# A gate chunk's last addition traced two groups behind its product, and transpositions of row sums two groups behind the sums

## The chip, the cores and the metric

The kernel runs on one core of a Trainium2 chip. The metric is the device time of one execution in microseconds: 983.66 us as the median of three executions (983.5 to 984.84).

## The reference, cut to what matters

A two-layer bidirectional encoder over one sequence of 512 tokens with a width of 1024, in fp32. Layer 0 (A here) mixes tokens with dilated sliding-window attention in three dilations and eight heads; layer 1 (B) with grouped-query attention, eight query heads on two key heads, rotary angles over a grid. Both layers attend with four more heads to 256 memory tokens.

```python
h = rmsnorm(x, norm_g[i])
proj = h @ w_in[i]                 # q, k, v heads, memory queries, gate path
o = concat(mixer(q, k, v), memory_attention(qm, mem_h, w_kv[i]))
y = o * silu(gate)
x = x + y @ w_out[i]
```

## The kernel before, in words

**Products.** Each fp32 product is made of three TensorE matmuls of rounded parts (mm3, L162 to L165: high by high, high by low, low by high). Weights come as blocks of 128 x 1024 by DMA (wl) and are split on the chip: ScalarE (ACT) casts the high part wh (L282), VectorE (DVE) subtracts it for the low part wo (L292), four blocks in a ring. Most projections multiply two-by-two blocks with seven products instead of eight, in the function s_chunk. Its products, in order, are 12, 11, S1, S2, S4, S3 and 22; each goes to a PSUM bank, and behind each a copy (keep, L357, on ACT) or an addition (add, L367, on DVE) takes the bank's sum out. One subtraction (L361) stands between: s5 minus s3 is the block 22 of the result, and s5's tile is where it is written; the last addition, of block 21, reads s3 and overwrites it.

**Order.** No scheduler moves anything: each engine runs its instructions in the order in which the program traces them. A Driver object counts groups. A group is twelve matmuls of 128 x 512 or twenty-four of 128 x 256 on one or two weight blocks. Behind a group's matmuls come, in this order, the first steps of the keep and add generators that are due (free), the splits, sums and loads of weights (advance, with its L292 and L282), the release of the group's own bank (with a delay d, counted in groups), and one step of every other running generator (tick). What follows an addition or a subtraction is a generator too, ev: for a gate block the tanh (ACT L722), the product with its argument (DVE L724), the load og of attention outputs from DRAM (L717), the multiplication (L732; for the memory heads' part L735, with a cast L738 and a subtraction L740). A chunk of n=256 (units = 1) has one group per product; there are eleven of them, among them the three gate chunks m, a and b of each layer. A chunk of n=512 has two groups per product.

**Around the change.** At the end of layer A, prep_y forms sums of the gated blocks (ys: L776, L778; yf: L784, L786) and splits them (yS: ACT L759, DVE L760) as right factors of the output projection (out_proj). The last heads' attention outputs are stored to DRAM by put_od (L915) and merged by their weights (L1062 to L1078; ACT's exponential L1067). The output projection's rows go through ev_o: residual and norm (L455), then the first factors of layer B. For its lower half of rows, sum_h (L496) makes the difference xs, and sums_h transposes it on PE (turn4, L461; splits L157 and L160) and makes three more sums (L504 to L506), which rest_h transposes later. The steps of ev_o are EO, in groups. The memory keys of layer B are normed (L519, L524, xn) and transposed (L531, qT) at the same time. In layer B the attention (attn_b: L1304, L1313, L1314, ptb L1323, pbT L1327 and L1332) runs between the groups of the gate chunks; its last outputs are stored to odb and loaded as og.

Of the kernel before, what the change touches and what calls it, by code (L numbers as in the profile page):

```python
# [13 lines left out]
ALU = mybir.AluOpType  # L14
# [12 lines left out]
MEM_STEP = 1, 1  # L27
MEM_D = 4
PD, W_EARLY = (1, 2, 2, 1), True
EO = 1, 2, 1, 1, 1  # L30
YB = {"m": (2, 2), "k": (1, 1, 1), 0: (1, 2, 1), 1: (1, 2, 1)}
Y = [3, 2, 2, 2, 3, 2, 2, 1, 1, 1]

# [91 lines left out]
def trunk_kernel(ctx: ExitStack, tc: tile.TileContext, x, mem, wall, norm_g, mem_norm_g, gcol,  # L125
                 qn_a, kn_a, qn_b, kn_b, ident_d, mask_d, tab_a, tab_b, out):
    nc = tc.nc
    V, A, G, T = nc.vector, nc.scalar, nc.gpsimd, nc.tensor
# [14 lines left out]
    def s2(dt=F32, name="s2"):  # L143
        return pool.tile([128, 512], dt, tag="s2", name=name, bufs=NS2)

    def pj(name="pj"):
        return psum.tile([128, 512], F32, tag="pj", name=name, bufs=4)
# [14 lines left out]
    def mm3(o, lh, ll, rh, rl, start, stop):  # L162
        T.matmul(o, lh, rh, start=start, stop=False, skip_group_check=True)  # L163
        T.matmul(o, lh, rl, start=False, stop=False, skip_group_check=True)  # L164
        T.matmul(o, ll, rh, start=False, stop=stop, skip_group_check=True)  # L165
# [183 lines left out]
    def s_chunk(n, act, ev, tokens=True, pre=None, half=False):  # L349


        units, per = n // 256, 1024 // n
        bank, snap = [None, None], {}

        def keep(name, u, b):
            t = snap[name, u] = s2(name="sn")
            A.copy(t, b)  # L357
            yield 1
            if name == "s3":
                c = snap["s5", u]  # L360
                V.tensor_tensor(c, c, t, ALU.subtract)  # L361
                yield 1
                yield from ev("22", u, c)

        def add(q, name, u, b):
            t = snap[name, u]
            V.tensor_tensor(t, b, t, ALU.subtract if q == "12" else ALU.add)  # L367
            yield 1
            yield from ev(q, u, t)

        after = ((keep, "z"), (add, "11", "z"), (keep, "s5"), (keep, "s2"), (add, "12", "s2"), (keep, "s3"), (add, "21", "s3"))
        for i, (a, s, fresh) in enumerate(PRODUCTS):
            while a not in act:
                drv.tick()
            if fresh:
                bank[s] = [pj() for _ in range(units)]
            for x in range(units):
                wh, wo = [t.rearrange("p (k c) -> p k c", c=n) for t in W.take()]
                ah, al = act[a][:, 0], act[a][:, 1]
                for b in range(2):  # L380
                    if pre and i == x == 0 and b:
                        pre()
                    if half and b:
                        n_half[0] += 1
                        if n_half[0] % half == 0:
                            drv.half()
                    o = bank[s][b] if units == 2 else bank[s][0][:, b * 256:(b + 1) * 256]
                    bs = slice(b * 128, (b + 1) * 128)
                    for k in range(per):
                        kk = x * per + k  # L390
                        st, sp = fresh and kk == 0 and (units == 2 or b == 0), kk == 3
                        if tokens:
                            mm3(o, ah[:, kk, bs], al[:, kk, bs], wh[:, k], wo[:, k], st, sp)
                        else:
                            mm3(o, wh[:, k, bs], wo[:, k, bs], ah[:, kk], al[:, kk], st, sp)
                drv.free()
                W.advance()
                if x == units - 1:
                    f, *arg = after[i]
                    for u in range(units):  # L400
                        d = 2 if f is keep else 2 + u + (units == 1 and i == 6)
                        drv.release(f(*arg, u, bank[s][u]), d)
                drv.tick()

# [35 lines left out]
    def norm_1(xb, both=False):  # L440

        ss = sm(2, "ss")
        for j in range(2):
            jk = s2(name="sq")
            if both and j:
                V.tensor_tensor_reduce(jk, xb[j], xb[j], 1.0 / 1024.0, 0.0, ALU.mult, ALU.add, ss[:, j:j + 1])
            else:
                A.activation(jk, xb[j], AF.Square, scale=1.0 / 32.0, accum_out=ss[:, j:j + 1])
        r, e = sm(1, "rstd"), sm(1, "mse")
        G.tensor_tensor(e, ss[:, 0:1], ss[:, 1:2], ALU.add)  # L450
        return rstd_of(e, 1)

    def norm_2(xb, r, row, js=(0, 1)):
        for j in js:
            V.scalar_tensor_tensor(xb[j], xb[j], r, row[j], ALU.mult, ALU.mult)  # L455
# [38 lines left out]
    def sum_h(low):  # L494
        s1 = s2(name="xs1")
        V.tensor_tensor(s1, low[0], low[1], ALU.subtract)  # L496
        return s1

    def sums_h(H, top, low, c, s1, sums):

        (a11, a12), a21 = top, low[0]
        s2_, s4 = s2(name="xs2"), s2(name="xs4")
        put_h(H, "S1", c, s1)
        V.tensor_tensor(s2_, s1, a11, ALU.subtract)  # L504
        V.tensor_tensor(a21, a11, a21, ALU.subtract)
        V.tensor_tensor(s4, a12, s2_, ALU.add)  # L506
        sums.append((s2_, s4, a21, low[1]))

    def rest_h(H, sums, d=1):
        for i, k in enumerate(("S2", "S4", "S3", "22")):  # L510
            for c in range(2):
                put_h(H, k, c, sums[c][i])
            yield d
# [187 lines left out]
    def gates(od, o_done):  # L701
# [3 lines left out]
        def gate(H, first, g, half=False):  # L705
# [6 lines left out]
            def ev(q, u, t):  # L712
# [29 lines left out]
                if {(2, 0, j), (2, 1, j)} <= y_done:  # L742
                    for k in range(2):
                        ys[2 * j + k] = (yt[j][0][:, k], yt[j][1][:, k])

            s_chunk(256, H, ev, tokens=False, half=half)

        def prep_y():
# [45 lines left out]
    def out_proj(YW, ys, src, evac, tiles, half=False):  # L794

        acc, done = {}, set()

        def load():
            for i in range(2):
                for u, t in enumerate(tiles()):  # L800
                    nc.sync.dma_start(t, src[2 * i + u])
                    acc[2 * i + u] = halves(t)
                yield 2

        def ev(q, u, t):
            b, n = 2 * (int(q[0]) - 1) + u, int(q[1]) - 1
            while b not in acc:
                yield 1
            V.tensor_tensor(acc[b][n], t, acc[b][n], ALU.add)
            done.add((n, b))  # L810

        drv.spawn(load(), ACC_AT)
        s_chunk(512, YW, ev, half=half)
        out_rest(ys, acc, done, evac)
# [89 lines left out]

    drv.spawn(mem_norm(0), MEM_AT)
    s_chunk(512, H, ev_v0, pre=second)
    km, vm = mem_kv(0, Ms[0])

# [256 lines left out]
    def ev_o(n, b, x1):  # L1165
        if n:
            for j in range(2):
                nc.sync.dma_start(x1d[b][:, j * 512:(j + 1) * 512], x1[j])
            r = norm_1(x1)
            yield EO[0]  # L1170
            norm_2(x1, r, rows["x1"])
            x1b[b] = x1
            yield EO[1]
            if b < 2:
                put_h(H2, "12", b, x1[1])
                put_h(H2, "11", b, x1[0])
            else:
                s1 = sum_h(x1)
                yield EO[2]
                sums_h(H2, x1b[b - 2], x1, b - 2, s1, sums_b)  # L1180
            if b == 3:
                yield EO[3]
                yield from rest_h(H2, sums_b, EO[4])

# [306 lines left out]
```

## Time and profile before

| | |
|---|---|
| time, median of three | 983.66 us |
| the profiled execution | 983.88 us |
| its span | 982.1 us |
| PE busy | 951.9 us (97%) |
| DVE busy | 822.1 us (84%) |
| ACT busy | 645.0 us (66%) |
| POOL busy | 333.5 us (34%) |
| DVE, L292, the low parts of weights | 255 x 1233 ns = 312.8 us |
| ACT, L282, the high parts | 255 x 1059 ns = 269.6 us |

Engines in the rows: PE is TensorE, DVE VectorE, ACT ScalarE, POOL GpSimd, SP the engine that issues most DMAs. A row of a timeline has start, duration, engine, line, operation, output and inputs, shapes, and in brackets the idle time before it with what ended it. A duration holds an instruction's whole passage, and the next one on DVE starts some 80 ns before its end. A row of waits has the total, the number and the longest. A row of stretches has the length, then the busy time and number of instructions of PE, PEld, DVE, ACT and POOL, the TensorE clock granted, the DMA share and GB/s.

### The profile page before, as it was taken

What the parts mean: (1) busy time and instruction counts of PE and PEld (TensorE: products, weight loads), DVE (VectorE), ACT (ScalarE), POOL (GpSimd) and SP (SyncE); (2) the same over time, 40 slices, a digit from 0 to 9 for tenths busy, and PEclk for the clock granted to TensorE, in tenths of its full rate; (3) what the DMA queues carried; (4) which work ended last, traced back from release to release, by engine and by line L of the source; (5) the groups of instructions that cost most, each with busy time, mean ns of one, the idle gap of its engine ahead of it and who ended that gap; (6) DMA issues with size and microseconds to landing.
All of it is one profiled execution on the core that took longest, in us unless ns stands there. A gap on an engine that the chain in (4) does not pass through costs nothing.

```text
span 982.1 us, 16662 instructions
## 1 busy us (share of the span) xinstructions
PE 951.9 (97%) x5724; PEld 838.8 (85%) x5724; DVE 822.1 (84%) x1487; ACT 645.0 (66%) x1623; POOL 333.5 (34%) x470
## 2 busy tenths in 40 slices
PE   7999999999999999999999989998999999998998
PEld 4788988888888888888899977886999999996886
DVE  6796788888888888888888998969689998889964
ACT  5555668686767676868676656455677766667650
POOL 1132423556555555554644010123533331011000
PEclk9999999999999999999999999999999999999999
DMA  8989947869686868686949795759695786786332
GB/s 333 309 275 351 239 97 188 290 120 268 154 250 155 250 164 243 158 249 137 271 117 300 228 235 173 258 218 322 181 204 144 196 213 171 227 213 152 129 129 86
DMA packets 86967, 206.13 MB, mean 210 GB/s; under 512 B 25058, under 2 KB 35810, under 8 KB 86883
## 3 DMA queue, kind: packets, MB, share of 16 engines
q1 hardware_dynamic: 70034, 146.28, 43.0%
q0 software_dynamic: 15552, 56.63, 30.5%
q10 hardware_dynamic: 1296, 2.16, 0.6%
q8 instruction: 45, 0.74, 0.3%
q14 instruction: 40, 0.32, 0.1%
HBM read 157.79 MB, written 12.65 MB: 174 GB/s over the span
## 4 chain that ended last, share of the span: by engine, by line
PE 77%; DVE 12%; DMA 6%; issue 2%; ACT 1%; POOL 1%; SPq 0%; DVEq 0%; POOLq 0%
PE pj L163 20%; PE pj L165 20%; PE pj L164 20%; DVE wo L292 3%; PE qT L531 2%; DMA wl<-in_wall_dram 1%; PE oo L1121 1%; PE sa L1019 1%; PE pt L1100 1%; PE sa L1015 1%; PE ptb L1323 1%; DMA od<-o 1%; PE xT L461 1%; DMA x1d<-acc 1%; DMA wl<-wl 1%
## 5 line engine op out<-in xcount | busy, mean ns | idle before, releaser
L292 DVE TENSOR_TENSOR wo<-wl,wh 128x1024 fp32r<-128x1024 f32 x255 | 312.8, 1233 | 10.3 <-ACT wh L282 10.0
L282 ACT CAST wh<-wl 128x1024 fp32r<-128x1024 f32 x255 | 269.6, 1059 | 73.5 <-PE pj L165 37.8
L163 PE MATMUL pj<-wh,hS 128*128 128x512 f32 (+1 forms) x448 | 164.5, 367 | 0.2 <-ACT sn L357 0.2
L164 PE MATMUL pj<-wo,hS 128*128 128x512 f32 (+1 forms) x448 | 157.9, 353 | 1.7 <-DVE wo L292 1.6
L165 PE MATMUL pj<-wh,hS 128*128 128x512 f32 (+1 forms) x448 | 158.2, 353 | 0.0
L163 PE MATMUL pj<-wh,h 128*128 128x512 f32 (+1 forms) x336 | 123.6, 368 | 0.7 <-ACT h L157 0.7
L164 PE MATMUL pj<-wo,h 128*128 128x512 f32 (+1 forms) x336 | 119.5, 356 | 2.1 <-DVE wo L292 2.1
L165 PE MATMUL pj<-wh,h 128*128 128x512 f32 (+1 forms) x336 | 119.6, 356 | 0.0
L410 POOL TENSOR_TENSOR rstd<-mse,half 128x4 f32<-128x4 f32 (+2 forms) x98 | 98.7, 1007 | 8.2
L164 PEld LDWEIGHTS pj<-wo,hS 128*128 128x128 f32 x448 | 85.0, 190 | 12.3 <-DVE wo L292 2.5
L165 PEld LDWEIGHTS pj<-wh,hS 128*128 128x128 f32 x448 | 84.7, 189 | 12.2
L163 PEld LDWEIGHTS pj<-wh,hS 128*128 128x128 f32 x448 | 84.8, 189 | 10.3 <-ACT sn L357 0.4
L357 ACT COPY sn<-pj 128x512 f32<-128x512 f32 x132 | 73.6, 590 | 18.0 <-PE pj L165 17.5
L409 POOL TENSOR_SCALAR mse<-hss 128x4 f32<-128x4 f32 (+1 forms) x86 | 46.1, 536 | 109.8 <-ACT junk L519 102.7
L519 ACT ACTIVATE junk<-sn 128x128 f32<-128x128 f32 x264 | 79.0, 307 | 0.2 <-DVE sn L361 0.2
L963 POOL TENSOR_TENSOR ta<-sn,tabs 128x128 f32<-128x128 f32 (+1 forms) x64 | 37.0, 579 | 121.1 <-DVE sn L524 81.7
L164 PEld LDWEIGHTS pj<-wo,h 128*128 128x128 f32 x336 | 64.4, 192 | 10.0 <-DVE wo L292 2.5
L165 PEld LDWEIGHTS pj<-wh,h 128*128 128x128 f32 x336 | 64.2, 191 | 9.3 <-DVE h L160 0.2
L163 PEld LDWEIGHTS pj<-wh,h 128*128 128x128 f32 x336 | 64.3, 191 | 8.4 <-ACT h L157 1.1
L367 DVE TENSOR_TENSOR sn<-pj,sn 128x512 f32<-128x512 f32 x99 | 67.4, 683 | 4.7 <-PE pj L165 4.4
L266 POOL DMA_DIRECT2D wl<-wl x33 | 29.3, 888 | 111.1 <-DVE wo L292 71.0
L163 PE MATMUL pj<-hS,wh 128*128 128x256 f32 x192 | 55.9, 291 | 0.0
(226 smaller groups left out, 2455.1 us busy)
## 6 DMA issues: line engine op xcount, KB each, us to landing
wl<-in_wall_dram SPq DMA_DIRECT2D x222, 512.0 KB, 6.9
wl<-wl POOLq DMA_DIRECT2D x66, 512.0 KB, 5.9
wl<-in_wall_dram POOLq DMA_DIRECT2D x42, 512.0 KB, 8.2
od<-o SPq DMA_DIRECT2D x12, 256.0 KB, 5.0
og<-od SPq DMA_DIRECT2D x12, 256.0 KB, 5.8
odb<-o SPq DMA_DIRECT2D x12, 256.0 KB, 3.4
og<-odb SPq DMA_DIRECT2D x12, 256.0 KB, 5.1
x<-in_x_dram SPq DMA_DIRECT2D x4, 512.0 KB, 5.6
```

Of the source, the lines that this page charges most:

```text
L163: T.matmul(o, lh, rh, start=start, stop=False, skip_group_check=True)
L164: T.matmul(o, lh, rl, start=False, stop=False, skip_group_check=True)
L165: T.matmul(o, ll, rh, start=False, stop=stop, skip_group_check=True)
L266: G.dma_start(self.tile[key], self.tile[c, "T2", x], accum_op=ALU.add)
L282: A.copy(wh, self.tile[self.items[i]])
L292: V.tensor_tensor(wo, self.tile[key], wh.bitcast(F32), ALU.subtract)
L357: A.copy(t, b)
L367: V.tensor_tensor(t, b, t, ALU.subtract if q == "12" else ALU.add)
L409: G.tensor_scalar(e, ss, EPS, None, ALU.add)
L410: G.tensor_tensor(r, e, half[:, 0:n], ALU.pow)
L519: A.activation(jk, p[:, j * 128:(j + 1) * 128], AF.Square, scale=QS, accum_out=ss[:, j:j + 1])
L963: G.tensor_tensor(ta[:, 0:n], xn[:, 0:n, 0:32], ropeA[:, 0, b, s0:s0 + n], ALU.mult)
```

## The change

In s_chunk the last addition (block 21) of a chunk of n=256 was released three groups behind its product, so that the subtraction L361, which follows two groups behind product S3's copy step, was traced before it overwrote s3. Now it is released two groups behind, as the others are, and the subtraction is in a function of its own that is called by whichever of the two comes first. The third number of EO, the groups between sum_h and sums_h, goes from 1 to 2: the transpositions of xs and the sums behind it come one group later. No instruction is added or taken away on any engine. Line numbers behind L357 grow by 7 (L361 is now L368, and lies in diff).

```diff
-EO = 1, 2, 1, 1, 1
+EO = 1, 2, 2, 1, 1
...
             if name == "s3":
-                c = snap["s5", u]
-                V.tensor_tensor(c, c, t, ALU.subtract)
+                diff(u)
                 yield 1
-                yield from ev("22", u, c)
+                yield from ev("22", u, snap["s5", u])
+
+        def diff(u):
+
+            if (u, "22") not in snap:
+                c = snap[u, "22"] = snap["s5", u]
+                V.tensor_tensor(c, c, snap["s3", u], ALU.subtract)
 
         def add(q, name, u, b):
             t = snap[name, u]
+            if name == "s3":
+                diff(u)
             V.tensor_tensor(t, b, t, ALU.subtract if q == "12" else ALU.add)
...
-                        d = 2 if f is keep else 2 + u + (units == 1 and i == 6)
+                        d = 2 if f is keep else 2 + u
```

**First place: DVE between layer A's last gate chunk and the output projection, before.** sn are the gate block's tiles, ys and yf the sums of prep_y, wo the weights' low parts; the first L367 is block 12 of gate chunk b.

```order
L724 SCALAR_TENSOR_TENSOR sn<-th,sn 128x512
L367 TENSOR_TENSOR sn<-pj,sn 128x512
L292 TENSOR_TENSOR wo<-wl,wh 128x1024
L776 TENSOR_TENSOR ys<-yf 128x512 x2
L778 TENSOR_TENSOR ys<-ys,yf 128x512 x2
L735 TENSOR_TENSOR sn<-sn,og 128x512
L292 TENSOR_TENSOR wo<-wl,wh 128x1024
L760 TENSOR_TENSOR yS_7129<-ys,yS_7129 128x512 x2
```

The same place after (L731 was L724, L739 was L732, L374 was L367, L783 and L785 were L776 and L778, L767 was L760, L742 was L735):

```order
L731 SCALAR_TENSOR_TENSOR sn<-th,sn 128x512
L292 TENSOR_TENSOR wo<-wl,wh 128x1024
L739 TENSOR_TENSOR yf<-sn,og 128x512 x2
L292 TENSOR_TENSOR wo<-wl,wh 128x1024
L783 TENSOR_TENSOR ys<-yf 128x512 x2
L785 TENSOR_TENSOR ys<-ys,yf 128x512 x2
L731 SCALAR_TENSOR_TENSOR sn<-th,sn 128x512
L374 TENSOR_TENSOR sn<-pj,sn 128x512
L292 TENSOR_TENSOR wo<-wl,wh 128x1024
L767 TENSOR_TENSOR yS_7096<-ys,yS_7096 128x512 x2
L742 TENSOR_TENSOR sn<-sn,og 128x512
L292 TENSOR_TENSOR wo<-wl,wh 128x1024
```

The two steps of ys stood behind the addition of block 12 and an L292; now the addition and that L292 stand behind them.

**The same stretch, some ten rows on, before**, with the chunk's last addition (the L367 here), the difference ahead of it, and the small steps that merge the last head (nmM, d):

```order
L784 TENSOR_TENSOR yf<-yf,ys 128x512 x2
L786 TENSOR_TENSOR yf<-yf 128x512 x2
L740 TENSOR_TENSOR y<-sn,y 128x2x256
L724 SCALAR_TENSOR_TENSOR sn<-th,sn 128x512
L361 TENSOR_TENSOR sn<-sn 128x512
L1062 TENSOR_TENSOR nmM<-stp,oth 128x8
L1064 TENSOR_TENSOR d<-nmM,stp 128x8
L1065 TENSOR_TENSOR d<-nmM,oth 128x8
L367 TENSOR_TENSOR sn<-pj,sn 128x512
L292 TENSOR_TENSOR wo<-wl,wh 128x1024
```

and after (L791, L793, L747 were L784, L786, L740; L1069 to L1072 were L1062 to L1065):

```order
L791 TENSOR_TENSOR yf<-yf,ys 128x512 x2
L793 TENSOR_TENSOR yf<-yf 128x512 x2
L368 TENSOR_TENSOR sn<-sn 128x512
L374 TENSOR_TENSOR sn<-pj,sn 128x512
L292 TENSOR_TENSOR wo<-wl,wh 128x1024
L767 TENSOR_TENSOR yS_7172<-yf,yS_7172 128x512 x2
L747 TENSOR_TENSOR y<-sn,y 128x2x256
L731 SCALAR_TENSOR_TENSOR sn<-th,sn 128x512
L1069 TENSOR_TENSOR nmM<-stp,oth 128x8
L1071 TENSOR_TENSOR d<-nmM,stp 128x8
L1072 TENSOR_TENSOR d<-nmM,oth 128x8
L292 TENSOR_TENSOR wo<-wl,wh 128x1024
```

The difference and the last addition went ahead of an L292, of L740 and L724, and of the small steps.

**Second place: PE at layer B's first operands, before.** xT is a transposition of a row sum (xs_7958 for the first quarter of rows, xs_8006 for the second), qT that of the normed memory key xn. These rows are the second quarter's transposition with its neighbours; the first quarter's stands thirteen rows earlier, with no qT.

```order
L164 MATMUL pj<-wo,act 128x512
L165 MATMUL pj<-wh,act 128x512
L461 MATMUL xT<-ident,xs_8006 128x128 x4
L531 MATMUL qT<-ident,xn 128x128 x4
L163 MATMUL pj<-wh,act 128x512
L164 MATMUL pj<-wo,act 128x512
```

and after, the first quarter's transposition (L468 was L461, L538 was L531):

```order
L164 MATMUL pj<-wo,act 128x512
L165 MATMUL pj<-wh,act 128x512
L468 MATMUL xT<-ident,xs_7958 128x128 x4
L538 MATMUL qT<-ident,xn 128x128 x4
L163 MATMUL pj<-wh,act 128x512
L164 MATMUL pj<-wo,act 128x512
```

The first quarter's transposition came a group later, to where the key's transposition stands; the second quarter's came a group later too.

**The same on DVE, before** (L455 is the norm's product, L496 the difference xs, L504 to L506 the three sums, hS the transposed parts):

```order
L455 SCALAR_TENSOR_TENSOR acc<-acc,rstd,row 128x512 x2
L496 TENSOR_TENSOR xs_7958<-acc 128x512
L292 TENSOR_TENSOR wo<-wl,wh 128x1024 x2
L160 TENSOR_TENSOR hS_7995<-xT,hS_7995 128x4x128
L504 TENSOR_TENSOR xs_7993<-xs_7958,acc 128x512
L505 TENSOR_TENSOR acc<-acc 128x512
L506 TENSOR_TENSOR xs_7994<-acc,xs_7993 128x512
L496 TENSOR_TENSOR xs_8006<-acc 128x512
L524 TENSOR_TENSOR xn<-pj,rstd 128x512
L160 TENSOR_TENSOR hS_7995<-xT,hS_7995 128x4x128
```

and after (L462, L503, L511 to L513, L531 were L455, L496, L504 to L506, L524):

```order
L462 SCALAR_TENSOR_TENSOR acc<-acc,rstd,row 128x512 x2
L503 TENSOR_TENSOR xs_7958<-acc 128x512
L292 TENSOR_TENSOR wo<-wl,wh 128x1024 x2
L503 TENSOR_TENSOR xs_7993<-acc 128x512
L531 TENSOR_TENSOR xn<-pj,rstd 128x512
L160 TENSOR_TENSOR hS_8031<-xT,hS_8031 128x4x128
L511 TENSOR_TENSOR xs_8029<-xs_7958,acc 128x512
L512 TENSOR_TENSOR acc<-acc 128x512
L513 TENSOR_TENSOR xs_8030<-acc,xs_8029 128x512
L531 TENSOR_TENSOR xn<-pj,rstd 128x512
```

The second difference and the first xn went ahead of the first quarter's split and three sums. In the same way, what starts behind a chunk's last part is traced a group earlier elsewhere: prep_y, and in layer B the attention with the memory and on the grid, down to the last heads' stores to odb.

## The prediction

> **What bounds the kernel now.** The page comes first, then the waits of TensorE (PE), then the busy time by stretches of the span.
>
> ```profile
> span 982.1 us, 16662 instructions
> PE 951.9 (97%) x5724; PEld 838.8 (85%) x5724; DVE 822.1 (84%) x1487; ACT 645.0 (66%) x1623; POOL 333.5 (34%) x470
> ```
> ```profile
> PE ob L164 <- DVE pbT L1332: 5.3, 3, 3.0
> PE pj L163 <- DVE sn L367: 4.4, 1, 4.4
> PE xT L461 <- DVE xs L496: 3.4, 2, 1.9
> PE pj L165 <- DVE y L740: 1.3, 1, 1.3
> ```
> ```profile
> 540.00:610.00 70.00, 64.78 (x433) 58.99 (x433) 67.11 (x122) 43.17 (x77) 6.05 (x7) 0.95 0.81 224
> 660.00:680.00 20.00, 15.95 (x85) 12.54 (x84) 17.07 (x24) 10.29 (x28) 8.45 (x10) 1.00 1.04 349
> 740.00:830.00 90.00, 89.13 (x719) 86.50 (x718) 87.06 (x155) 61.68 (x168) 24.13 (x29) 1.00 0.71 182
> 880.00:912.00 32.00, 26.73 (x161) 23.45 (x160) 31.79 (x54) 21.96 (x42) 4.35 (x5) 0.96 0.66 158
> 912.00:982.00 70.00, 64.86 (x321) 54.13 (x319) 49.84 (x78) 28.52 (x49) 0.00 (x0) 0.99 0.33 117
> ```
>
> PE is busy for 951.9 of 982.1 us, so a gain can only come out of its 30.2 us of idle time, and a loss is any new idle time. The rows of waits (line: us in all, times, longest) name 14.4 us of it, and each stands where the change reorders VectorE (DVE). The stretches (first PE, PEld, DVE, ACT, POOL busy, then granted clock) tell the two kinds of places apart: in 540 to 610, 740 to 830 and 880 to 912 DVE is busy for 67.11 of 70, 87.06 of 90 and 31.79 of 32 us, so what counts there is **which instruction stands ahead of which in DVE's queue**. In 660 to 680 and behind 912 both engines have room, and what counts is how far one step follows another.
>
> No instruction is added or removed, on any engine. All terms below are shifts. They are summed against the profiled execution, 983.88 us beside a median of 983.66.
>
> **Place A: the end of layer A's gates, 570 to 600.** Here is a row of the chain of waits, then DVE, ACT and PE in order of time, then a stretch with its granted clock:
>
> ```profile
> 564.77 10.67 DMA od<-o
> ```
> ```profile
> 572.40 1.21 DVE L292 TENSOR_TENSOR wo<-wl,wh 128x1024 fp32r<-128x1024 f32 x1
> 573.53 1.28 DVE L776 TENSOR_TENSOR ys<-yf 128x512 f32<-128x512 f32 x2
> 575.53 1.29 DVE L778 TENSOR_TENSOR ys<-ys,yf 128x512 f32<-128x512 f32 x2 [0.72 <-DMA od<-o]
> ...
> 585.04 0.68 DVE L724 SCALAR_TENSOR_TENSOR sn<-th,sn 128x512 f32<-128x512 f32 x1
> 585.64 0.68 DVE L361 TENSOR_TENSOR sn<-sn 128x512 f32<-128x512 f32 x1
> ...
> 586.59 0.68 DVE L367 TENSOR_TENSOR sn<-pj,sn 128x512 f32<-128x512 f32 x1
> ```
> ```profile
> 586.71 0.21 ACT L1067 ACTIVATE e<-d 128x16 f32<-128x16 f32 x1 [6.12 <-DVE d L1065]
> ```
> ```profile
> 576.21 0.40 PE L164 MATMUL pj<-wo,y 128*128 128x512 f32 x1
> ```
> ```profile
> 585.10:591.80 6.70, 4.47 (x11) 3.51 (x12) 5.70 (x11) 5.09 (x10) 0.97 (x2) 0.50 1.06 294
> ```
>
> PE's 4.4 us wait ends with the L367 that ends at 587.27 (586.59 + 0.68): it reads the last gate's bank, which the output projection wants next. From start to start an L292 costs 1.13 us (572.40 to 573.53) and a 128x512 step 0.60 (585.04 to 585.64). After the change one L292 (1.13), one L724 and one L740 (0.60 each) and three small steps of L1062 to L1065 (together 0.33, the rest of 0.95 between 585.64 and 586.59 less 0.60) stand behind that L367 instead of ahead of it. Taken alone this is 1.13 + 1.20 + 0.33 = 2.66 us gained.
>
> But preparing y moves forward as well, because the gates' last parts come a group earlier. L776 and L778 then stand ahead of L724, the L367 of the product 12, and the L292 that was at 572.40. L778 must wait for the od store, which was issued at 564.77 and landed at 575.44 (10.67 later): its tile takes the store's slot. Without the three steps ahead of it (1.13 + 0.60 + 0.60 = 2.33) DVE is there 2.3 us sooner, and SP's store isn't: the idle time grows from 0.72 to about 3.05 us. DVE is a strict queue in this reading, so all behind L778 pays. After it (576.7) come L724, L367 and L292, and the L292 ends at 576.7 + 0.60 + 0.60 + 1.13 = 579.05. PE needs it at 576.21: **a new wait of about 2.85 us**. The next split comes after yS, L735 and L292 (1.20 + 0.60 + 1.13) at 582.0, which is nearly in time; the next one is behind yS, L784, L786 (1.20 each), L361, L367 (0.60 each) and its own 1.13, at 587.9, where PE had its split in time before and waited for the bank alone. The awaited L367 itself ends near 586.8, so its gain has gone to 0.5 us. The small steps come at about 590.5 instead of 586.24 to 586.59, behind that L292, yS, L740 and L724. ACT's exponential at 586.71 waits for them, and behind it ACT holds the casts on which the next yS and L292 wait; an estimate from these rows is 1.7 us more of DVE idle time. DVE is then late by 2.33 + 1.7 = 4.0 us, in a stretch where it has 2.9 us in 70 to spare, so PE is late by that: **+4.0 us**. Bounds: −2.7 (no stall at L778) and +5 (the second wait is not shared with the first).
>
> Around and behind the 4.4 us wait the granted clock is 0.50 (585.10 to 591.80). [...]
>
> **Place EO: layer B's first operands, 660 to 680.** PE and DVE in order of time:
>
> ```profile
> 667.11 0.39 PE L165 MATMUL pj<-wh,act 128*128 128x512 f32 x1
> 669.05 0.63 PE L461 MATMUL xT<-ident,xs 128*128 128x128 f32 x4 [1.56 <-DVE xs L496]
> 669.43 0.48 PE L163 MATMUL pj<-wh,act 128*128 128x512 f32 x1
> 669.75 0.40 PE L164 MATMUL pj<-wo,act 128*128 128x512 f32 x1
> 669.99 0.40 PE L165 MATMUL pj<-wh,act 128*128 128x512 f32 x1
> ...
> 674.33 0.63 PE L461 MATMUL xT<-ident,xs 128*128 128x128 f32 x4 [1.88 <-DVE xs L496]
> ```
> ```profile
> 662.10 1.42 DVE L455 SCALAR_TENSOR_TENSOR acc<-acc,rstd,row 128x512 f32<-128x512 f32 x2 [2.52 <-DMA x1d<-acc]
> ...
> 668.22 0.68 DVE L496 TENSOR_TENSOR xs<-acc 128x512 f32<-128x512 f32 x1
> 668.83 2.35 DVE L292 TENSOR_TENSOR wo<-wl,wh 128x1024 fp32r<-128x1024 f32 x2
> ...
> 674.10 0.68 DVE L524 TENSOR_TENSOR xn<-pj,rstd 128x512 f32<-128x512 f32 x1
> ```
>
> Each transposition now follows its difference by a further group of twelve matmuls, 12 x 0.235 = 2.8 us at the pitch of 669.75 to 669.99. Both waits (1.56 and 1.88) go. What is late next is xn: it is now traced on PE beside the first transposition, and DVE makes it behind L496, two L292 and the second L496, at 668.83 + 2.27 + 1.20 = 672.3. PE gets there at 667.11 + 0.23 + 2.87 + 0.38 = 670.6, a wait of 1.7: the group behind a transposition takes 0.32 (669.43 to 669.75) and eleven pitches, 2.87 in all, and the transposition 0.38 (669.05 to 669.43). The next group then ends at 672.3 + 0.6 + 2.87 = 675.8, against 674.93 + 0.4 + 2.87 = 678.2 before: **−2.3 us**. Bounds: 0, if rstd for xn or another split is later than I see, and −3.4, both waits gone. DVE's 2.52 us wait for the x1d landing can also swallow a part of a delay from place A: −0.5 (−1 to 0).
>
> **Layer B's gates and attention, 740 to 912.** The attention's steps now start one group earlier. On PE this takes a group of 2.7 to 2.9 us out from before each pbT that PE waits for; on DVE it takes out one L292 (1.13) and in places also a 0.60 step or two (to 2.4). The waits of PE between 740 and 830 alone have this row:
>
> ```profile
> PE ptb L1323 <- DVE pbT L1332: 0.3, 1, 0.3
> ```
>
> In 880 to 912 PE waited 5.3 us for pbT in three waits. PE comes 2.7 to 2.9 us of work sooner to it and the L1332 only 1.13 to 2.4 sooner. Mid-way 2.85 − 1.4 gives **+1.45 us** (bounds −1, if the later group is absorbed in a wait behind it, and +3). In 740 to 830 PE had 0.87 us without work in 90, but it did wait for pbT there, so it has no lead at that place, and 2.85 − 1.13 = 1.7 us is taken. An estimate of what shows of it, with some given back at the waits that were there: **+1.0 us** (bounds −0.5 and +2.5).
>
> **The end, behind 912.**
>
> ```profile
> 953.01 1.33 DVE L735 TENSOR_TENSOR sn<-sn,og 128x512 f32<-128x512 f32 x2 [3.80 <-DMA og<-odb]
> ```
>
> The last odb store comes a group (2.7 us) sooner, and so does the og load for which DVE waits 3.8 us. PE's 1.3 us wait for y L740, with its gap of 1.5 in all, goes: **−1.5 us** (bounds −1.5 and 0). The bunched gate steps elsewhere (two tanh, two L724, two L732 in a tick instead of one) lie under PE, which is busy throughout from 45 to 540:
>
> ```profile
> 45.00:540.00 495.00, 494.92 (x2756) 427.51 (x2755) 410.02 (x829) 353.43 (x1005) 241.35 (x352) 1.00 0.78 215
> ```
>
> They cost nothing, with a 0.60 step either way as bounds; without that cover a bunched pair makes what follows it on DVE 0.60 late.
>
> **Sum:** 4.0 − 2.3 − 0.5 + 1.45 + 1.0 − 1.5 = +2.15 us. 983.88 + 2.15 = 986.0 in a profile, and 985.8 as a median.
>
> **The rivals.**
> 1. *No stall at L778.* The store's 10.67 us is long for it; the page's median issue to landing is in this row:
> ```profile
> od<-o SPq DMA_DIRECT2D x12, 256.0 KB, 5.0
> ```
> If the new order of og loads (in pairs) lets it land by 572.4, place A gives its 2.66 us. Against it: DMA is no less asked for there. Time: 983.66 − 2.7 − 2.3 + 2.45 − 1.5 = 979.6.
> 2. *The clock stays up.* If the 4.4 us wait falls into pieces none of which halves the clock, the 11 matmuls of the row 585.10 to 591.80 cost 0.235 instead of up to twice that: at most 2.6 us back; with 2 of them the time is 983.8. Against it: the third split alone, at 587.9, still makes a wait of about 3 us.
> 3. *Slower by more.* Place A at +5, place EO at 0 since xn or a split takes the place of xs, and layer B at +2.45: 983.66 + 5 + 2.45 − 1.5 = 989.6. It decides if xn is later than 674.5. For it: DVE is busy for 17.07 of 20 us there.
> 4. *The other side of place A by itself:* were the added wait no longer than the old one, A is 0 and the time 981.8, inside the bound of no change.
>
> **How the numbers follow.** A measurement of this kernel can tell about 0.2% (2.0 us) from no change: below 981.7 is faster, above 985.6 slower. My forecast, 985.8 with 983.5 to 988.5 for itself, has 0.42 (of it 0.30 slower and 0.12 same); rival 1 has 0.27 (faster); rivals 2 and 4 together 0.13 (same 0.12, faster 0.01); rival 3 has 0.18 (slower). That makes faster 0.28, same 0.24, slower 0.48. The range takes in most of rivals 1 and 3: 979.0 to 989.5.
>
> **What would show it.** Right: a wait of about 3 us of L778 for od<-o, PE waiting for L292 near 576, no wait for xs at 669 and one for xn instead, no wait for y L740 at the end. Wrong: L778 without a wait (rival 1); PE's clock at full between 585 and 592 (rival 2); xs or xn waits of over 3 us (rival 3). The forecast fails if the od store lands elsewhere than at 575, since one DMA's landing carries the largest term.

## The result, and the profile after

The changed kernel takes 989.16 us (median of 6, 986.52 to 992.04), against 983.70 before (median of 6, 982.45 to 984.84). The ratio is 1.0057, with a 95% interval of 1.0043 to 1.0070: **slower by some 5.6 us**. The sign is the forecast one and the time lies in the stated range, but the forecast's own size was +2.15 us. The profiled execution took 988.84 us.

Its page:

```profile
span 987.1 us, 16669 instructions
PE 952.2 (96%) x5724; PEld 839.5 (85%) x5724; DVE 824.7 (84%) x1487; ACT 644.8 (65%) x1623; POOL 336.5 (34%) x470
```

The work is the same (PE 951.9 to 952.2 us busy), so nearly all of the 5.0 us of span is idle time. The waits of PE after (line: us in all, times, longest), to be held against those of before:

```profile
PE pj L164 <- DVE wo L292: 10.0, 5, 3.1
PE ob L164 <- DVE pbT L1339: 4.9, 3, 3.1
PE ptb L1330 <- DVE pbT L1339: 3.2, 1, 3.2
PE qT L538 <- DVE xn L531: 2.7, 1, 2.7
...
PE pj L163 <- DVE sn L374: 1.7, 3, 0.7
PE om L164 <- DVE pmT L667: 1.1, 1, 1.1
```

The 4.4 us for L367, the waits for xs and that for y L740 are gone. New are the waits for wo (4.4 us in all before), for xn, for pmT, and the 3.2 us of ptb. Where they lie shows in the stretches; PE's idle time is a stretch's length less the first busy time. Before:

```profile
500.00:562.00 62.00, 62.00 (x522) 61.80 (x521) 55.55 (x117) 42.33 (x101) 19.99 (x29) 1.00 0.81 232
562.00:645.00 83.00, 77.78 (x416) 66.42 (x416) 74.93 (x113) 45.83 (x73) 8.75 (x11) 0.96 0.69 202
645.00:735.00 90.00, 85.71 (x603) 79.04 (x602) 69.71 (x91) 57.04 (x134) 36.87 (x43) 1.00 0.86 249
735.00:850.00 115.00, 114.13 (x915) 110.70 (x915) 108.30 (x193) 79.82 (x211) 27.86 (x32) 1.00 0.73 190
850.00:935.00 85.00, 79.72 (x517) 72.10 (x516) 78.89 (x136) 57.00 (x111) 7.80 (x9) 0.98 0.65 171
935.00:970.00 35.00, 33.70 (x163) 28.01 (x163) 24.39 (x34) 12.10 (x18) 0.00 (x0) 1.00 0.29 104
```

After:

```profile
500.00:562.00 62.00, 60.99 (x509) 60.38 (x508) 54.31 (x113) 40.69 (x99) 19.61 (x29) 1.00 0.82 230
562.00:645.00 83.00, 76.17 (x415) 64.79 (x414) 73.44 (x113) 47.51 (x75) 9.18 (x12) 0.98 0.68 203
645.00:735.00 90.00, 86.69 (x607) 80.60 (x606) 73.33 (x95) 56.86 (x136) 37.92 (x42) 1.00 0.82 240
735.00:850.00 115.00, 110.40 (x869) 107.66 (x869) 104.73 (x185) 76.78 (x205) 26.62 (x33) 0.97 0.70 184
850.00:935.00 85.00, 79.47 (x543) 72.08 (x542) 77.98 (x135) 55.40 (x108) 8.37 (x9) 1.00 0.69 181
935.00:970.00 35.00, 35.00 (x173) 29.39 (x172) 28.11 (x42) 16.97 (x26) 0.00 (x0) 1.00 0.27 91
```

PE's idle time goes from 0 to 1.0 us in 500 to 562, from 5.2 to 6.8 in 562 to 645 (place A), from 4.3 to 3.3 in 645 to 735 (place EO), **from 0.9 to 4.6 in 735 to 850**, from 5.3 to 5.5 in 850 to 935, and from 1.3 to 0 at the end. The largest new idle time is not at place A, where the prediction had its largest term, but in layer B. DVE, too, is less busy there than before (104.73 against 108.30 us of 115): it waits itself.

A fixed stretch of time holds other work in a kernel that runs late. The second way to compare is over the same work: from the 976th to the 1323rd of PE's 1360 products of L163 into pj, which has the same matmuls in both kernels, before and after:

```profile
720.07:950.53 230.46, 224.08 (x1635) 210.58 (x1634) 211.19 (x360) 155.90 (x352) 40.32 (x46) 0.99 0.68 180
721.78:957.11 235.33, 225.20 (x1635) 211.65 (x1634) 209.62 (x357) 154.89 (x350) 38.07 (x46) 0.99 0.68 179
```

Layer B's gates and attention take 4.9 us longer (230.46 to 235.33).

**What DVE waits for.** Rows after, engine by engine (SP's queue, GpSimd, ACT, ACT's last square of a head, GpSimd again, DVE, PE). SP's rows start with the first store of a memory head and the loads of weights behind it:

```profile
752.39 0.33 SPq L1221 DMA_DIRECT2D odb<-o  x1
752.82 0.37 SPq L233 DMA_DIRECT2D wl<-in_wall_dram  x1
761.90 0.33 SPq L1221 DMA_DIRECT2D odb<-o  x1
762.33 0.88 SPq L233 DMA_DIRECT2D wl<-in_wall_dram  x2
770.61 0.33 SPq L1221 DMA_DIRECT2D odb<-o  x1
```
```profile
780.35 0.94 POOL L256 DMA_DIRECT2D wl<-wl  x1 [2.00 <-DMA wl<-in_wall_dram]
```
```profile
791.58 1.05 ACT L282 CAST wh<-wl 128x1024 fp32r<-128x1024 f32 x1 [3.02 <-DMA wl<-wl]
```
```profile
788.16 0.31 ACT L526 ACTIVATE junk<-sn 128x128 f32<-128x128 f32 x1
```
```profile
792.25 0.87 POOL L266 DMA_DIRECT2D wl<-wl  x1 [10.04 <-DVE wo L292]
793.18 0.23 POOL L416 TENSOR_SCALAR mse<-hss 128x4 f32<-128x4 f32 x1
793.49 1.04 POOL L417 TENSOR_TENSOR rstd<-mse,half 128x4 f32<-128x4 f32 x1
```
```profile
794.57 0.69 DVE L531 TENSOR_TENSOR sn<-sn,rstd 128x512 f32<-128x512 f32 x1 [2.54 <-POOL rstd L417]
```
```profile
808.22 1.11 PE L1330 MATMUL ptb<-ident,pb 128*128 128x128 f32 x4 [3.19 <-DVE pbT L1339]
```

The same place of SP's queue before:

```profile
754.06 0.33 SPq L1214 DMA_DIRECT2D odb<-o  x1
754.48 2.39 SPq L233 DMA_DIRECT2D wl<-in_wall_dram  x2
764.00 0.33 SPq L1214 DMA_DIRECT2D odb<-o  x1
```

In these rows SP issues in its order, and a store waits for PE's and ACT's output of a head (L1221 for ACT's copy o, L683: 35.5 us in four waits of 740 to 800 after). Before, two loads stood between the first store and the second; now it is one, since the memory heads start a group earlier and the ring of blocks lets a load go by groups. The other load is behind the second store, 9.5 us later (752.39 to 761.90), and each load after it is one place late. GpSimd's adding DMA (L256) then waits for the block (2.00 us), and ACT's cast for the sum (3.02). The squares from which GpSimd makes rstd stand ahead of that cast, not behind it: the last one starts at 788.16. What holds rstd up is GpSimd's own queue. Its next adding DMA, L266, reads the same sum and a block that DVE has split; it goes out at 792.25, and L416 and L417, which make rstd, stand behind it until 794.53. For that DVE waits (2.54). In the profiles of two experiments below (e4 and e6) the wait of L266 ends with the landing of the sum itself (9.65 and 10.00 us).

### The profile page after: what moved, and what is told of

Read it like the earlier page. It is cut to its first block, busy times and chain, and to the rows that moved or that the text cites. A ratio compares the mean times of both kernels' runs of the same rounds, so it can differ in the third digit from the quotient of the medians.

```text
span 987.1 us, 16669 instructions
## 1 busy us (share of the span) xinstructions
PE 952.2 (96%) x5724; PEld 839.5 (85%) x5724; DVE 824.7 (84%) x1487; ACT 644.8 (65%) x1623; POOL 336.5 (34%) x470
## 5 line engine op out<-in xcount | busy, mean ns | idle before, releaser
L292 DVE TENSOR_TENSOR wo<-wl,wh 128x1024 fp32r<-128x1024 f32 x255 | 313.6, 1235 | 9.9 <-ACT wh L282 9.5
L163 PE MATMUL pj<-wh,hS 128*128 128x512 f32 (+1 forms) x448 | 164.4, 367 | 0.6 <-DVE sn L374 0.6
L163 PE MATMUL pj<-wh,h 128*128 128x512 f32 (+1 forms) x336 | 123.4, 367 | 1.0 <-ACT h L157 1.0
L417 POOL TENSOR_TENSOR rstd<-mse,half 128x4 f32<-128x4 f32 (+2 forms) x98 | 104.6, 1068 | 8.2
L163 PEld LDWEIGHTS pj<-wh,hS 128*128 128x128 f32 x448 | 84.8, 189 | 10.5 <-DVE sn L374 0.8
L357 ACT COPY sn<-pj 128x512 f32<-128x512 f32 x132 | 73.6, 591 | 13.6 <-PE pj L165 13.2
L416 POOL TENSOR_SCALAR mse<-hss 128x4 f32<-128x4 f32 (+1 forms) x86 | 42.9, 499 | 104.3 <-ACT junk L526 100.1
L266 POOL DMA_DIRECT2D wl<-wl x33 | 29.6, 896 | 124.1 <-DVE wo L292 58.6
L163 PEld LDWEIGHTS pj<-wh,h 128*128 128x128 f32 x336 | 64.2, 191 | 8.8 <-ACT h L157 1.4
L374 DVE TENSOR_TENSOR sn<-pj,sn 128x512 f32<-128x512 f32 x99 | 67.5, 684 | 4.9 <-PE pj L165 4.3
L163 PE MATMUL pj<-hS,wh 128*128 128x256 f32 x192 | 57.1, 297 | 1.1 <-DVE sn L374 1.1
```

What stands on the lines that cost most here:

```text
L266: G.dma_start(self.tile[key], self.tile[c, "T2", x], accum_op=ALU.add)
L292: V.tensor_tensor(wo, self.tile[key], wh.bitcast(F32), ALU.subtract)
L416: G.tensor_scalar(e, ss, EPS, None, ALU.add)
L417: G.tensor_tensor(r, e, half[:, 0:n], ALU.pow)
```

## The experiments

Each kernel's edit is given against the changed kernel. The experiments are numbered e1 to e12 in the order in which they stand. A set EARLY names the 256-wide chunks whose last addition comes a group earlier, in the order 0 qm, 1 m, 2 a, 3 b (layer A), 4 qm, 5 kv, 6 and 7 the queries, 8 m, 9 a, 10 b (layer B); in the others it stays three groups behind:

```diff
+        late = 0
+        if units == 1:
+            late = n_chunk[0] not in EARLY
+            n_chunk[0] += 1
...
-                        d = 2 if f is keep else 2 + u
+                        d = 2 if f is keep else 2 + u + (late and i == 6)
```

Changes in us below are the ratio to the kernel before, on the same chip, times 983.4. Each profile is of one execution. A table at the end of this section compares all of them over the same work.

### EO alone

```diff
+    EARLY = ()
```

> Only the third number of EO is 2; every chunk's last addition stays three groups behind. Theory 1, the places add: PE's two waits for xs (1.72 and 2.04 us of idle time) go and one for xn of 1.7 to 2.9 us comes, so 0.9 to 2.3 us are gained: 981.4 to 982.8. Rival: the delay of layer A was merely absorbed by the wait for x1d in the changed kernel, and the transpositions gain nothing by themselves: 983.7.

982.67 us; ratio 0.9994 (0.9984 to 1.0003), −0.6 us (−1.6 to +0.3): below what theory 1 wanted, and not told from nothing. PE's idle time in 645 to 735 is 2.7 us against 4.3 before, but that doesn't show a gain: it is 2.9 and 3.0 us in the profiles of e10 and e12, whose EO is as before:

```profile
645.00:735.00 90.00, 87.33 (x621) 81.37 (x620) 72.35 (x94) 58.79 (x143) 35.20 (x44) 1.00 0.88 258
```

### The chunks alone

```diff
-EO = 1, 2, 2, 1, 1
+EO = 1, 2, 1, 1, 1
```

> Only the last additions of the 256-wide chunks come a group earlier; EO is as before. Theory 1, the places add: the changed kernel's 989.2 and the 0.9 to 2.3 us that EO gives: 990.1 to 991.5. Rival: the two parts meet, since EO moves layer B's start against the weights' DMAs and so makes the loss in layer B: 987 or less.

992.52 us; ratio 1.0094 (1.0081 to 1.0107), +9.2 us. The whole loss is in this part, and EO takes some of it back: the changed kernel is at +5.6, so that EO is worth 3.6 us here and 0.6 alone. Why was not found.

### Layer A's chunks alone, layer B's alone

```diff
-EO = 1, 2, 2, 1, 1
+EO = 1, 2, 1, 1, 1
+    EARLY = (0, 1, 2, 3)
```

> The last addition comes earlier in layer A's four 256-wide chunks alone, EO as before. By the lag of PE's matmuls between the two profiles, the changed kernel is 3.1 us late at 605 us, of which 0.3 is from the start. Theory 1: up to 2.8 us slower, of which the wait for x1d (2.5 us on DVE at 662) may take 1 to 2: 984.7 to 986.5. Rival, all comes from layer B: 983.7.

988.93 us; ratio 1.0058 (1.0045 to 1.0072), +5.7 us, more than either side expected. What differs from the changed kernel's profile is DVE at place A; its row, then the stretches:

```profile
576.76 1.29 DVE L790 TENSOR_TENSOR ys<-ys,yf 128x512 f32<-128x512 f32 x2 [3.84 <-DMA od<-o]
```
```profile
500.00:562.00 62.00, 61.01 (x510) 60.49 (x509) 54.24 (x113) 41.51 (x101) 20.03 (x29) 1.00 0.80 230
562.00:645.00 83.00, 74.09 (x393) 62.99 (x392) 71.49 (x110) 44.21 (x70) 8.78 (x11) 0.96 0.69 203
```

The second step of ys waits 3.84 us for the od store, and PE is idle for 8.9 us of 562 to 645.

```diff
-EO = 1, 2, 2, 1, 1
+EO = 1, 2, 1, 1, 1
+    EARLY = (4, 5, 6, 7, 8, 9, 10)
```

> The last addition comes earlier in layer B's seven 256-wide chunks alone, EO as before. By the lag of PE's matmuls the changed kernel loses some 8.5 us between 680 and 835 us and wins back some 4 behind 880. Theory 1, these are layer B's own: 983.7 + 4 to 5 = 987.7 to 988.7. Rival, the loss between 680 and 835 us comes from a weight DMA that lands late by the luck of one execution, or from what layer A moves: 983.7 less what the end gives, 981 to 983.

988.02 us; ratio 1.0053 (1.0040 to 1.0066), +5.2 us. Layer B has a loss of its own of the same size, and no luck of one execution: this profile has ACT's wait for wl (2.4 us) and the wait of ptb (3.2 us) again.

### Layer A's last gate chunk as before; layer B's second query chunk as before

```diff
+    EARLY = (0, 1, 2, 4, 5, 6, 7, 8, 9, 10)
```

> The changed kernel, but layer A's last gate chunk (b) keeps its last addition three groups behind. Theory: all of layer A's loss (5.7 us when layer A alone was changed) comes from this one chunk, by the wait of L785 for the od store and by the splits behind it. Then 983.3 + 4.7 (layer B alone) - 0.6 (EO alone) = 987.4, and PE has its one wait of about 4.5 us near 587 again. Rival: the loss is spread over the four chunks, or EO had already won it back in the changed kernel: 989.

991.29 us; ratio 1.0070 (1.0049 to 1.0090). The theory fell: in time nothing came back. The sums ys wait for chunk a, not for b; this profile has the wait for the od store (3.55 us) all the same.

```diff
+    EARLY = (0, 1, 2, 3, 4, 5, 6, 8, 9, 10)
```

> The changed kernel, but the second query chunk of layer B keeps its last addition three groups behind. Theory: the 3.3 us wait of ptb for pbT near 808 and the half clock behind it come from this chunk's blocks 22 and 21 in one step, whose norm and rotation (L531, L1262, L1263, 1.93 us) stand twice ahead of that pbT. Then this wait goes and 3 to 5.5 us come back: 983.7 to 986.2. Rival: the attention's earlier start makes the wait, whatever its own chunk does: 989.

987.80 us; ratio 1.0051 (1.0038 to 1.0065), not told apart from the changed kernel. PE's idle time in 735 to 850 is 4.5 us:

```profile
735.00:850.00 115.00, 110.52 (x881) 106.53 (x881) 106.16 (x187) 78.00 (x206) 28.05 (x33) 1.00 0.72 187
```

The wait of ptb is cut into pieces, and the clock stays at 1.00. The 3 to 5.5 us of the theory didn't come back in time. But idle time doesn't show what a halved clock costs, since PE counts as busy in it: for 3.30 of 3.30 us in the changed kernel from 808.30 to 811.60, with 16 matmuls at a granted clock of 0.50. Over the same work (third column of the table) this profile lost 2.4 us, not 4.9, and only 0.7 of the difference is idle time; the rest is busy time, 223.47 us for 225.20. So a share of two heads in one step and of the half clock behind the long wait is not excluded.

### A tile of its own for the first ys

```diff
-            jk = small.tile([128, 128], F32, tag="junk", name="junk", bufs=2)
+            jk = small.tile([128, 128], F32, tag="junk", name="junk", bufs=1)
...
+            G.memset(s2_[0][:, 0:8], 0.0)
+            s2_[0] = pool.tile([128, 512], F32, tag="ysx", name="ys", bufs=1)
```

> The changed kernel with a tile of its own for the first result of L785, so that it doesn't wait for the od store (two small fills on GpSimd hold the old slot, and the ACT scratch tile has one buffer for two). Theory: the wait of L785 is part of layer A's loss; where it was 3.1 to 3.8 us long, PE lost 5.5 to 6.2 us by 605 us, where it was 0.4 us, 2.8. Without it layer A's loss is about 2.8 in every execution: 989.2 - 1 to 2.5 = 986.7 to 988.2, and less spread over the runs. Rival, the store's wait is hidden and the splits' order alone costs: 989.

991.17 us; ratio 1.0072 (1.0053 to 1.0090): not faster. In its profile L785 waits for nothing and PE's idle time in 562 to 645 is 7.0 us, less than the 8.9 with a wait of 3.84, but not less than the 6.8 of the changed kernel with 0.41. The wait for the store is not the main part of layer A's loss, or something in the edit took it back: the fills that stand in GpSimd's queue until the store has landed (a wait of 6.8 us), or the scratch tile with one buffer, with which ACT is busy for 666.4 us instead of 644.8. This run can't tell which.

### Layer B's gate chunks alone, with EO

```diff
+    EARLY = (8, 9, 10)
```

> EO as changed, and the last addition earlier in layer B's three gate chunks alone. By the lag of PE's matmuls, layer B alone lost about 5.5 us between 680 and 833 us, which holds the query chunks, 0 to 1.4 between 880 and 912 and won 2.4 to 3.2 behind. Theory, the gain of the end belongs to the gate chunks: 982.7 (EO alone) - 3 to -1 = 979.7 to 981.7, below both kernels. Rival, the gates' earlier parts make the loss around 800 too: above 983.3.

984.11 us; ratio 1.0004 (0.9994 to 1.0013). No loss near 800 and no gain at the end: its profile has PE's wait for y L752 at 958.83 still (1.3 us). So the gates alone don't make the end's gain; it is there in every profile in which most of layer B's chunks ahead of the gates are early too.

### The memory heads' stores out of SP's queue

```diff
-        nc.sync.dma_start(od_b[i], t)
+        (nc.scalar if i >= 8 else nc.sync).dma_start(od_b[i], t)
```

> The changed kernel, but the four odb stores of the memory heads are issued by ACT, behind its own copy of the output, and no longer stand in SP's queue ahead of the loads of weights. New theory: with the memory heads a group earlier, SP issues one load (before: two) between the first store and the second; every later load is then one store of some 8.7 us late, ACT's cast near 790 waits 3.0 us for its block (2.4 to 3.0 in all kernels with layer B changed), DVE 1.9 to 3.4 us for rstd behind it, and PE 3.3 us for pbT. Then 3 to 6 us come back: 983 to 986, and no cast waits for wl between 780 and 800. Rival: PE is a group early against a busy DVE, whatever the loads do: 989.

987.96 us; ratio 1.0043 (1.0026 to 1.0059), +4.2 us: less than the changed kernel's by 1.4 us, with intervals that overlap, and less than was expected. The profile shows the mechanism. No cast waits for wl in 745 to 850, and PE's waits in 735 to 850 are

```profile
PE ptb L1330 <- DVE pbT L1339: 1.2, 1, 1.2
PE om L164 <- DVE pmT L667: 1.1, 1, 1.1
```
```profile
735.00:850.00 115.00, 112.77 (x913) 110.17 (x912) 108.71 (x191) 80.79 (x213) 26.42 (x33) 1.00 0.75 189
```

Its idle time there is 2.2 us, against 4.6 in the changed kernel and 0.9 before. So in these profiles 2.4 of the 3.7 us went with the late loads. Over the same work layer B lost 1.8 us here and 4.9 in the changed kernel. What stays is likely PE's being a group early against DVE; that was only argued. This execution had layer A's long store wait (3.27 us), as others had, and was the longest of its twelve (992.42).

The control is the kernel before with the same edit (EARLY empty, EO as before).

> The kernel before with the same four stores issued by ACT: the control. New theory: the loads that were late cost it nothing, since PE has 1.8 us idle or slow between 735 and 850: 983 to 984. Rival: the stores' place costs ACT or SP by itself: off by over 1 us.

983.82 us; ratio 1.0001 (0.9990 to 1.0012): the stores' place costs nothing by itself.

```diff
+    EARLY = (4, 5, 6, 7, 8, 9, 10)
...
-        nc.sync.dma_start(od_b[i], t)
+        (nc.scalar if i >= 8 else nc.sync).dma_start(od_b[i], t)
```

> EO as changed, the last additions earlier in layer B alone, the four stores issued by ACT. New theory: without layer A's loss and without the late loads what is left is the gain of the end (1.5 us) and EO's 0.6: 983.7 - 2 = 981 to 983, below both kernels. Rival: layer B's earlier attention costs its 4.7 us still: 987.

982.24 us; ratio 0.9989 (0.9973 to 1.0004), −1.1 us. With layer B early and the stores in SP's queue, +5.2; with EO and the stores on ACT, −1.1. Between these two kernels both EO and the stores change, and EO was worth 0.6 us alone but 3.6 with the chunks early. So the stores' share in time is 2.7 to 5.7 us by this pair, and 1.4 by e9 against the changed kernel, where the stores alone differ. The theory holds in direction; the size in time stays open. This profile still has 1.3 us of ACT's wait for wl and a wait of 2.5 us of ptb, with 3.6 us idle in the stretch:

```profile
735.00:850.00 115.00, 111.42 (x886) 108.60 (x885) 106.39 (x188) 76.09 (x197) 25.48 (x32) 0.99 0.73 188
```

It is the fastest kernel here by its median, below the changed one beyond the intervals, and not told apart from the one before.

### Chunk a alone

```diff
-EO = 1, 2, 2, 1, 1
+EO = 1, 2, 1, 1, 1
+    EARLY = (2,)
```

> Only layer A's second gate chunk (a) has its last addition a group earlier, EO as before. New theory of layer A: the sums ys wait for this chunk's last part, and so it alone puts L776 and L778 ahead of the splits and the addition: by the stretches of the profiles, 562 to 645 loses 3 to 5 us of PE, and the 1.5 us near 536 to 540, which are the first chunks', don't come: 983.7 + 3 to 5 = 986.7 to 988.7. Rival: it takes all four chunks: under 985.

983.96 us; ratio 1.0013 (0.9999 to 1.0026), +1.3 us. The theory of layer A fell for the most part: chunk a alone gives 0 to 2.6 us of 5.7. Its profile (of the shortest of its twelve executions, 982.09 to 987.66) has the ys early, a wait of 0.32 us for the store, and splits for which PE waits, but PE's idle time is hardly more than before (5.4 us):

```profile
562.00:645.00 83.00, 77.63 (x409) 66.00 (x408) 75.07 (x114) 46.56 (x73) 8.76 (x11) 0.96 0.69 203
```

Which other chunk makes the rest with it was not tried.

### All profiles over the same work

The rows of e9 and e11 for the work that took 230.46 us before and 235.33 in the changed kernel:

```profile
728.43:960.70 232.27, 224.12 (x1636) 210.55 (x1634) 210.16 (x358) 155.90 (x351) 38.32 (x46) 0.99 0.69 181
719.05:950.54 231.49, 223.15 (x1635) 210.41 (x1634) 209.71 (x357) 155.29 (x350) 38.30 (x46) 0.99 0.70 182
```

The table has the change against the kernel before, in us. Each column runs from one product of L163 into pj to another, at the times that they have in the kernel before; ahead of both lie the same matmuls in every kernel.

| profile | place A, 535.27 to 610.38 | place EO, 645.60 to 720.07 | layer B, 720.07 to 950.53 | the end, from 950.53 |
|---|---|---|---|---|
| changed kernel | +3.1 | −1.4 | +4.9 | −1.6 |
| e1, EO alone | +0.9 | −1.7 | −0.6 | −0.4 |
| e2, chunks alone | +6.2 | +0.7 | +5.2 | −1.6 |
| e3, layer A's chunks | +6.5 | +0.4 | −0.1 | −0.3 |
| e4, layer B's chunks | −0.8 | +0.3 | +6.0 | −1.6 |
| e5, without chunk b | +4.3 | +0.5 | +5.0 | −1.6 |
| e6, without the second query chunk | +5.8 | −2.4 | +2.4 | −1.6 |
| e7, a tile for ys | +4.4 | +0.5 | +5.2 | −1.6 |
| e8, layer B's gates and EO | +0.9 | −0.7 | +0.7 | +0.2 |
| e9, stores on ACT | +7.8 | +0.7 | +1.8 | −1.6 |
| e10, control | −0.2 | −1.6 | −0.1 | −0.2 |
| e11, layer B, EO, stores on ACT | +0.1 | −1.2 | +1.0 | −1.6 |
| e12, chunk a alone | +0.9 | −1.7 | 0.0 | −0.1 |

Layer B loses 4.9 to 6.0 us in the five profiles that have all its chunks early and the stores in SP's queue, and 1.0 and 1.8 with the stores on ACT. The control, and all kernels with layer B's chunks as before, lie between −0.6 and 0.0. So of 5 to 6 us in the profiles 3 to 5 go with the stores' queue. Place EO can't be told: −2.4 to +0.7 us with the change of EO, −1.7 to +0.7 without it.

## Why the prediction was right or wrong

**The total: in the range, but not as forecast.** 989.16 us lies outside the 983.5 to 988.5 that the forecast gave for itself, and next to rival 3's 989.6, for whose sake the range went up to 989.5. Rival 3 was to be decided by xn later than 674.5, and xn came at 674.72; but its wait was 2.69 us, not over 3, and layer B lost more than its +2.45, by a cause that neither the forecast nor a rival had. That the time fell inside the range is luck in part.

**Place A, +4.0 us: right in kind, +2.6 in the changed kernel's profile** (idle time of 500 to 562 and of 562 to 645 together), and +5.7 us in time with layer A alone, somewhat over the bound of 5. Over the same work it is +3.1 in the changed kernel, and 5.8 to 7.8 us in the four other profiles with the same chunks of layer A early and ys in the store's slot (e2, e3, e6, e9). DVE there, after:

```profile
574.42 1.29 DVE L785 TENSOR_TENSOR ys<-ys,yf 128x512 f32<-128x512 f32 x2 [0.41 <-DMA od<-o]
...
576.84 1.21 DVE L292 TENSOR_TENSOR wo<-wl,wh 128x1024 fp32r<-128x1024 f32 x1
...
585.31 0.69 DVE L374 TENSOR_TENSOR sn<-pj,sn 128x512 f32<-128x512 f32 x1
585.92 1.21 DVE L292 TENSOR_TENSOR wo<-wl,wh 128x1024 fp32r<-128x1024 f32 x1
```

The split that was to come at 587.9 ended at 587.13, and PE waited 3.1 us for it: the wait for L292 took the place of that for L367, as worked out. The forecast wait of about 3 us for the od store came in those four profiles (3.06, 3.84, 3.14 and 3.27 us) and in e5's (3.55), and was 0.41 in this one, where the store landed sooner (574.42 against 575.44). Rival 1 had this landing as its point of decision and a gain of 2.7 us behind it; that was wrong, since with hardly a wait the splits' order cost 2.6 all the same. The 1.0 us in 500 to 562 was put at nothing, under PE's cover to 540: 0.71 of it lies at 536.99, where PE waits for a bank (L374), just where the quoted stretch ends; with chunk a alone it isn't there.

**Place EO, −2.3 and −0.5 us: right in kind, the size not shown.** The waits for xs (1.56 and 1.88) are gone and one for xn is there, of 2.69 us for the forecast 1.7, as rstd is late by 0.94, which was the named bound. By these waits 0.75 us are gained:

```profile
675.55 0.63 PE L538 MATMUL qT<-ident,xn 128*128 128x128 f32 x4 [2.69 <-DVE xn L531]
```
```profile
674.72 0.69 DVE L531 TENSOR_TENSOR xn<-pj,rstd 128x512 f32<-128x512 f32 x1 [0.94 <-POOL rstd L417]
```

By idle time the stretch gained 1.0 us here and 1.6 with EO alone, but 1.3 in e10 and e12 too, whose EO is as before. The times say 0.6 alone, not told from nothing, and with the chunks' change as the base 9.2 − 5.6 = 3.6. The wait for the x1d landing fell from 2.5 to 1.3 us, but it was 0.9 with chunk a alone, so that it took up a delay from place A is not shown.

**Layer B, 740 to 830, +1.0 us: the step that failed.** It counted PE's and DVE's shift and left out SP's queue, that is, it put what the stores do to the loads at nothing. The attention with the memory moves a group earlier, and its stores with it; they pass a load, and the loads behind them wait. PE's new idle time was 3.7 us, outside the bound of +2.5, and 2.4 of it went when the stores left SP's queue. The 1.4 us that are left are near the +1.0 that was worked out for the shift alone. Over the same work this term and the next, +2.45 together, came out as +4.9, and as +1.8 and +1.0 with the stores on ACT. That the loss is in layer B and goes for the most part with the stores' queue is shown; the steps between the late loads and the wait of ptb are read off one profile and its like.

**880 to 912, +1.45 us: too high by idle time.** In 850 to 935 it rose by 0.2 us, and by 1.1 with layer B alone. That PE was late already, so that DVE had caught up, is likely, but only argued.

**The end, −1.5 us: right**, 1.3 us of idle time gone, and 1.6 over the same work; with the gates alone it didn't go.

**Rival 2**, the clock at full between 585 and 592, didn't come: behind the wait of 3.1 us it was 0.67 (587.30 to 591.00). Which waits leave the clock up no run shows: it was 0.50 behind 2.99 us at 909.35 in the kernel before (909.40 to 912.60) and 1.00 behind 3.10 us at 914.16 in the changed one. In layer B the clock doesn't set the size of the loss alone: e6 lost 2.4 us at a mean clock of 1.00, the changed kernel 4.9 at 0.99 and e9 1.8 at 0.99.

So the sum of +2.15 us came out as 1.0 + 1.6 − 1.0 + 3.7 + 0.2 − 1.3 = 4.2 us of idle time; the rest of the 5.0 us of span lies outside these stretches and in PE's busy time. Over the same work it is 3.1 − 1.4 + 4.9 − 1.6 = 5.0.

## What to carry to other kernels

When a step is traced earlier, list what it issues on each queue, and for a DMA that waits for a computation, which transfers stand behind it there: a store that moves ahead of one load can make all later loads late by one store (here those at 752.39 and 761.90 stand 9.5 us apart). A gain read off one wait holds only until the next instruction in that queue is looked at; here the bank's wait of 4.4 us became a wait of 3.1 us for a split. A tile slot that is shared with a store ties an engine's queue to a landing that differs from one execution to the next (8.0 to 10.9 us here, in three profiles with the same layer A up to the store). Where one kernel runs late against another, compare them over the same work: a fixed stretch of time showed 1.0 us less in layer B for e11 than for the changed kernel, the same work 3.8.

## What the runs showed of the hardware

The od store's landing differs by executions. From its issue at 566.2 to 566.3 it took 8.0 us in the changed kernel, 10.7 with the chunks alone (e2) and 10.9 with the memory heads' stores on ACT (e9), three kernels that are the same up to there. It was 10.67 us in the kernel before and 11.46 with layer A's chunks alone (e3). The times of the changed kernel spread over 5.5 us, where those before had 2.4; that this landing makes the spread was not shown.

Waits of about the same length had different clocks behind them. Behind the 3.19 us wait at 808 and the 3.1 us wait at 914 of the changed kernel:

```profile
808.30:811.60 3.30, 3.30 (x16) 3.30 (x17) 3.26 (x6) 2.63 (x6) 0.00 (x0) 0.50 1.04 179
...
914.30:917.60 3.30, 3.30 (x22) 3.04 (x23) 3.26 (x7) 1.40 (x5) 0.00 (x0) 1.00 0.13 25
```

The granted clock is 0.50 and 1.00. A lower clock stood behind shorter waits too: 0.50 behind one of 2.99 us at 909.35 in the kernel before (909.40 to 912.60), 0.61 in the 3.3 us behind a wait of 1.89 us at 678.69 with layer A's chunks alone, 0.70 behind one of 1.88 us at 679.69 with the chunks alone, while it was 1.00 behind 1.88 us at 674.33 in the kernel before, and behind 2.82 us at 600.10 in the changed one (600.20 to 603.60). What decides it was not found.
